# Layer 1's scores of a query pair in five score banks and one run of 1280 columns per unit, and another start for the planner's clock

## The chip, the cores and the metric

The kernel runs on one core of one Trainium2 chip. The metric is the device time of one execution in microseconds. The core has five engines that run at the same time and hand work to each other through semaphores: PE (TensorE, matmuls), DVE (VectorE), ACT (ScalarE), POOL (GpSimd) and SP (SyncE, which here issues all DMAs). PSUM, where PE writes its results, has eight banks of 512 fp32 columns by 128 partitions.

## The reference

A diffusion transformer of two layers over 1024 latent tokens and 256 context tokens, width 1024, all in fp32. Layer 0 is attention in a neighbourhood with a bias, layer 1 is full attention with 16 query heads that share 4 key and value heads; after each stands a SwiGLU block of hidden width 2816. Cut to layer 1's mixer, which the change touches:

```python
def qknorm_gqa_mixer(h_lat, h_ctx, w_qkv, q_gain, k_gain, w_o, ang_row, ang_col, with_ctx_out):
    q, k, v = project_qkv(h_lat, w_qkv, GQA_HEADS, GQA_KV_HEADS)      # 16 and 4 heads of 64
    qc, kc, vc = project_qkv(h_ctx, w_qkv, GQA_HEADS, GQA_KV_HEADS)
    q = axial_rope(rms_norm(q, q_gain), ang_row, ang_col)
    k = axial_rope(rms_norm(k, k_gain), ang_row, ang_col)
    kc = rms_norm(kc, k_gain)
    k_all = jnp.concatenate([kc, k], axis=1)                          # 256 + 1024 keys
    v_all = jnp.concatenate([vc, v], axis=1)
    ...
    s = jnp.einsum('bqhgd,bshd->bhgqs', q_b, k_all).astype(jnp.float32) * scale
    p = jax.nn.softmax(s, axis=-1).astype(v_all.dtype)
    return jnp.einsum('bhgqs,bshd->bqhgd', p, v_all)
```

Layer 1 is the last one, so its context tokens give keys and values alone.

## The kernel before

**Products in two parts.** Every operand of a matmul is split into a high part, rounded to the fast fp32r format, and a low part, the rest. A projection (`dense`, lines 782 to 784) is three matmuls per 128 input columns: high by high, high by low, low by high. The names `wh`, `wl` are the parts of a weight, `ah`, `al` those of an activation. ACT makes the high part (line 219) and POOL or DVE the low part (line 209).

**Stages.** A start-up (to about 128 us in the profile) whose order is written by hand with times; layer 0's projections, attention and output projection (to about 850 us); layer 0's SwiGLU (to 1765 us); layer 1's norm and its key and value projections; layer 1's attention (1866 to 2568 us), with the query projections and the output projection of the first 512 tokens between; layer 1's SwiGLU (to the end).

**What sets the order.** From the end of the start-up on, a planner (`Sim`) writes the program. Each piece of work is a generator that yields the letter of an engine (P, A, D, G or S) when it wants to issue. The planner has a clock of its own, a cost for each instruction (`cost`, `LAT`), a time for each engine from which it is free (`free`) and one for the DMAs (`dma_end`). It gives an engine that is free by its clock to the waiting generator of the lowest line number; the attention has lines 1 and 2, the projections come through `pump` on line 9 and so take PE when nothing of the attention wants it. `Slots.take` and `Slots.back` hand out buffers by that clock. On the chip only the order on each engine remains, and the semaphores. Before, PE counted as busy until 20 us after the planner's start (`p0=20000.0`, in ns) and the DMAs as free from its start.

**Layer 0's opening.** The planner's part begins while PE works on the last value projection of the start-up (line 716). SP then issues masks, the rows for the modulation, key and query tiles of head 0 (`K`, `Qs`, lines 1158 to 1169), `Vt`, the bias `braw`, a weight and the modulation's weights `adaw`. PE's work is the scores (line 1237), the projections of the next two heads (782 to 784), whose weights are already there, the transposes of the probabilities (1261) and the products with the values (1282). DVE adds the bias and finds the extreme (1244), and sums the modulation (752).

**Layer 1's attention.** The work is tiled into pairs: one head and 256 queries, two units of 128 queries. There are 64 pairs: two blocks of 512 queries by 16 heads by two. For a pair before:

- `ctx_scores` (1527, 1528): the scores against the 256 context keys, both units into one bank `X`, and one reduction over it for both maxima (1530).
- `scores1` (1538, 1539), twice per unit: 512 keys into a bank of `S`, of which there are two, and a reduction (1541). The query tile `Q` holds high over low; the keys lie in two tiles, high over low (`k1`) and low over high (`k2`), and the two matmuls against them give all four products.
- `unit1`: DVE takes the extreme of the three maxima (1550); ACT takes the exponential in three pieces of 512, 512 and 256, each with its sum (1556); DVE adds the three sums (1563) and inverts (1565); POOL scales the 1280 probabilities in `Pt` (1567).
- `part`, three times per unit: PE transposes 2 or 4 blocks of 128 into a bank of `T`, of which there are three (1574); ACT copies the high part into `pT` (1580); DVE subtracts for the low part (1582).
- `weigh1`: per unit ten matmuls (1605) of the values `V`, whose 128 columns are high and low part, with the 256 columns of `pT`, high beside low, into the unit's half of the one bank `o`.
- `gather` (815 to 825): ACT copies the parts on other partitions (817, 820), DVE adds in two steps (823, 825) into `z`.

The last bank, `ps`, is that of the projections. So the eight banks are three `T`, one `X`, two `S`, one `o`, one `ps`. SBUF holds two query tiles, four key tiles, two value tiles, three `Pt`, two `pT`, four `z`, two `o32`, two `xr`. After the attention `out_split` loads its output back and splits it (`ah`, `al`, lines 800 and 802), and the SwiGLU stage's first matmuls (`pm`) need all of it.

## Time and profile before

| | |
|---|---|
| median of 3 runs | 3374.49 us (3369.88 to 3377.92) |
| the profiled execution's own time | 3373.64 us |
| its span, first to last instruction | 3371.9 us |
| mean granted TensorE clock | 0.982 |
| PE, DVE, ACT, POOL busy | 94%, 58%, 40%, 29% of the span |

In the profile's rows a line such as `L1541 DVE TENSOR_REDUCE nm<-Sb ... x256 | 170.0, 684 | 59.0 <-PE ...` gives source line, engine, operation, output and inputs, count, busy time in us, mean duration of one in ns, and the engine's idle time before it with what ended it. Matmul durations overlap, so what a matmul costs is the distance between starts and not its duration. A row of the windows gives start and end, length, then for each engine busy time and count, the granted clock as a share, the share of the DMA engines and GB/s.

### The profile page before, as it was taken

The numbers are of one execution on the slowest core, as the hardware profiler recorded it, in microseconds if no ns is written. First come the engines' busy times: TensorE is split into PE (matmuls) and PEld (weight loads), VectorE is DVE, ScalarE is ACT, GpSimd is POOL, SyncE is SP. The second block draws the span as 40 slices with busy tenths as digits, with TensorE's granted clock in tenths as the row PEclk, the third lists the DMA queues.
The fourth block names the chain that finished last, engine by engine and source line by source line (L and its number), as shares of the span: only waits on it lengthen the run. The fifth ranks groups of instructions, "written<-read, shape, count | busy, mean of one in ns | idle before, by whom it ended". The sixth has DMA issues, their size and how long they took to land. (4 is left out here: it accounts for less than half of the span.)

```text
span 3371.9 us, 47168 instructions
## 1 busy us (share of the span) xinstructions
PE 3157.7 (94%) x17352; PEld 2690.8 (80%) x17352; DVE 1949.0 (58%) x3843; ACT 1335.5 (40%) x2915; POOL 968.4 (29%) x807
## 2 busy tenths in 40 slices
PE   7699999988999999999998998889887999999998
PEld 5688899867888888888886777678776788888887
DVE  7587975655665533333365777887887333333335
ACT  4254555543311111111134777777775311211223
POOL 4243543343211011000035554324334211110112
PEclk8899999999999999999999999999999999999999
DMA  7766755554333311111115233213211211111111
GB/s 242 209 198 200 225 177 167 173 163 151 122 119 120 127 39 38 38 42 40 38 39 179 93 119 88 57 56 93 74 49 60 75 44 38 63 50 38 49 57 57
DMA packets 177591, 337.98 MB, mean 100 GB/s; under 512 B 29904, under 2 KB 80336, under 8 KB 175312
## 3 DMA queue, kind: packets, MB, share of 16 engines
q1 hardware_dynamic: 177360, 334.96, 31.6%
q8 instruction: 137, 2.24, 0.3%
q14 instruction: 94, 0.77, 0.1%
HBM read 267.78 MB, written 70.64 MB: 100 GB/s over the span
## 5 line engine op out<-in xcount | busy, mean ns | idle before, releaser
L209 POOL TENSOR_TENSOR wl<-wr,wh 128x512 fp32r<-128x512 f32 x214 | 293.7, 1378 | 1186.4 <-ACT wh L219 1182.1
L956 ACT ACTIVATE sa<-pa 128x512 f32<-128x512 f32 (+1 forms) x110 | 61.0, 555 | 734.3 <-PE pa L784 734.2
L993 PE MATMUL pm<-hh,woh 128*128 128x512 f32 (+1 forms) x912 | 330.1, 362 | 0.0
L994 PE MATMUL pm<-hl,woh 128*128 128x512 f32 (+1 forms) x912 | 329.5, 361 | 0.0
L995 PE MATMUL pm<-hh,wol 128*128 128x512 f32 (+1 forms) x912 | 329.3, 361 | 0.0
L1004 DVE SCALAR_TENSOR_TENSOR h<-pm,modB,h 128x512 f32<-128x512 f32 (+1 forms) x368 | 242.1, 662 | 148.1 <-PE pm L995 147.6
L783 PE MATMUL pa<-al,wh 128*128 128x512 f32 (+1 forms) x880 | 324.9, 369 | 2.9 <-POOL al L336 1.8
L782 PE MATMUL pg<-ah,wh 128*128 128x512 f32 (+1 forms) x880 | 325.1, 369 | 0.0
L782 PE MATMUL pa<-ah,wh 128*128 128x512 f32 (+1 forms) x880 | 325.0, 369 | 0.0
L784 PE MATMUL pa<-ah,wl 128*128 128x512 f32 (+1 forms) x880 | 324.5, 369 | 0.0
L783 PE MATMUL pg<-al,wh 128*128 128x512 f32 (+1 forms) x880 | 324.4, 369 | 0.0
L784 PE MATMUL pg<-ah,wl 128*128 128x512 f32 (+1 forms) x880 | 324.0, 368 | 0.0
L219 ACT CAST wh<-wr 128x512 fp32r<-128x512 f32 x334 | 203.5, 622 | 255.6 <-PE pg L783 101.9
L970 DVE TENSOR_TENSOR sa<-sa,pg 128x512 f32<-128x512 f32 (+1 forms) x110 | 69.6, 633 | 365.6 <-PE pg L784 365.5
L1567 POOL TENSOR_SCALAR Pt<-Pt,rc 128x1280 f32<-128x1280 f32 x128 | 177.4, 1386 | 327.4 <-PE Tb L1574 231.0
L1605 PE MATMUL ob<-pT,V 128*128 128x256 f32 x1280 | 202.3, 296 | 55.1 <-DVE z L825 21.0
L752 DVE CUSTOM_DVE_ANT_0 adaj<-adaw,crow 128x512 f32<-128x512 f32 x256 | 207.9, 812 | 73.3 <-DMA adaw<-in_adaT 70.9
L209 DVE TENSOR_TENSOR wl<-wr,wh 128x512 fp32r<-128x512 f32 x120 | 96.1, 803 | 265.4 <-ACT wh L219 265.0
L1605 PEld LDWEIGHTS ob<-pT,V 128*128 128x128 f32 x1280 | 169.7, 191 | 83.1 <-ACT pT L1580 25.4
L1580 ACT CAST pT<-Tb 128x512 fp32r<-128x512 f32 (+1 forms) x384 | 182.8, 521 | 103.1 <-PE Tb L1574 99.4
L1582 DVE TENSOR_TENSOR pT<-Tb,pT 128x512 fp32r<-128x512 f32 (+1 forms) x384 | 212.0, 590 | 6.8 <-ACT pT L1580 4.1
L1541 DVE TENSOR_REDUCE nm<-Sb 128x1 f32<-128x512 f32 x256 | 170.0, 684 | 59.0 <-PE Sb L1539 58.6
(273 smaller groups left out, 7693.0 us busy)
## 6 DMA issues: line engine op xcount, KB each, us to landing
wr<-in_fin SPq DMA_DIRECT2D x88, 512.0 KB, 3.5
adaw<-in_adaT SPq DMA_DIRECT2D x160, 256.0 KB, 3.7
wr<-in_wqkv SPq DMA_DIRECT2D x53, 512.0 KB, 4.6
wr<-in_fout SPq DMA_DIRECT2D x44, 512.0 KB, 3.5
wr<-in_wo SPq DMA_DIRECT2D x32, 512.0 KB, 4.0
K<-Kd SPq DMA_DIRECT2D x32, 320.0 KB, 5.5
Qs<-Qd SPq DMA_DIRECT2D x80, 128.0 KB, 4.3
Vt<-Vd SPq DMA_DIRECT2D x16, 640.0 KB, 5.7
```

The costliest lines, as they stand in the source:

```text
L209: (g if self.engine == "G" else v).tensor_tensor(lo[:, c], raw[:, c], hi[:, c].bitcast(F32), ALU.subtract)
L219: s.copy(hi[:, c], raw[:, c])
L752: v.tensor_tensor_reduce(junk[:], aw[:], crow[w][:, c * 512:c * 512 + 512], 1.0, 0.0, ALU.mult, ALU.add, raw[:, m, w, c:c + 1])
L782: t.matmul(ps, lhsT=hi[:, c], rhs=ah[:, kc, :n], start=kc == 0, stop=False)
L783: t.matmul(ps, lhsT=hi[:, c], rhs=al[:, kc, :n], start=False, stop=False)
L784: t.matmul(ps, lhsT=lo[:, c], rhs=ah[:, kc, :n], start=False, stop=kc == KC - 1)
L993: t.matmul(ps[:, :n], lhsT=hi[:, c], rhs=hh[:, cols], start=i == 0, stop=False)
L994: t.matmul(ps[:, :n], lhsT=hi[:, c], rhs=hl[:, cols], start=False, stop=False)
L995: t.matmul(ps[:, :n], lhsT=lo[:, c], rhs=hh[:, cols], start=False, stop=i == 1)
L1004: v.scalar_tensor_tensor(h, ps[:, :n], self.g2(m, b), h, ALU.mult, ALU.add)
L1582: v.tensor_tensor(pT[:, i0:i0 + n, P:], Tv, pT[:, i0:i0 + n, :P].bitcast(F32), ALU.subtract)
L1605: t.matmul(o[:, p * 256:p * 256 + 256], lhsT=pair.hd.kv.V[:, kb, :], rhs=pT[:, i, :], start=i == 0, stop=i == 9)
```

## The change

It has two parts.

*The planner's start.* `p0` becomes 3000 and `d0`, new, tells the planner that the DMAs are taken up to 15 us after its start.

*Layer 1's attention.* One tile `S5` of five banks holds a pair's scores. Columns 0 to 1023 are unit 0's own keys, 1024 to 1279 its context keys, 1280 to 1535 unit 1's context keys, 1536 to 2559 its own keys, so that each unit has a run of 1280 columns and the middle bank holds the context scores of both. One reduction and one exponential with its sum serve a unit. The planner treats the tile as three parts: `scores_[0]` and `scores_[1]` are given back after the exponential of their unit, `scores_[2]`, the middle, after the second. The query tile now holds high over low and low over high side by side, and the key tile exists once; the two matmuls take the two query copies against the same keys. The other three banks, `B`, serve transposes, results, projections and the means of the norms; a projection takes one during the attention only where two are idle. Transposes put both units' high parts side by side and their low parts beside them (`pT`, and `pt` for the last two blocks), and the product adds high and low side in the same 256 columns, 2 matmuls per block of keys, 20 per pair as before; it begins when all six pieces of both units are there. The gather is one copy and one addition. Before layer 1's attention its projections use the five banks one by one (`banks["S"]`).

```diff
-CFG = dict(lag=3, tv=8.0, tm=5.0, t1=43.0, t2=58.0, p0=20000.0)
+CFG = dict(lag=3, tv=8.0, tm=5.0, t1=43.0, t2=58.0, p0=3000.0, d0=15000.0)
...
         bg.free.update(P=CFG["p0"])
+        bg.dma_end = CFG["d0"]
...
+    def bank1():
+
+        slots = banks["B" if live["att"] else "S"]
+        while len(slots.idle) < (2 if live["att"] else 1):
+            yield ""
+        return slots, slots.idle.pop(0)
...
+                    pair.S = yield from scores_[0].take()
+                    bg.enter("att", own_scores(pair, 0), 1)
+                    yield from scores_[2].take()
                     bg.enter("att", ctx_scores(pair), 1)
+                    yield from scores_[1].take()
+                    bg.enter("att", own_scores(pair, 1), 1)
                     for p in range(2):
+                        bg.enter("att", unit1(pair, p), 2)
                     bg.enter("att", weigh1(pair), 2)
 
+    def scores1(pair, p, d, sl):
+        for i in range(2):
+            t.matmul(pair.S[:, d:d + sl.stop - sl.start], lhsT=pair.q[p][:, i], rhs=pair.hd.kv.k[:, sl], start=i == 0, stop=i == 1)
...
+    def unit1(pair, p):
+        S = pair.S[:, 1280 * p:1280 * p + 1280]
...
         yield "D"
+        v.tensor_reduce(rc[:, 0:1], S, AX.X, ALU.max, negate=True)
         Pt = yield from A1["Pt"].take()
+        yield "A"
+        s.activation(Pt[:], S, AF.Exp, bias=rc[:, 0:1], accum_out=rc[:, 1:2])
+        scores_[p].back(pair.S)
         pair.x -= 1
         if not pair.x:
+            scores_[2].back(pair.S)
...
+        T = yield from banks["B"].take()
...
+        hi = pT[:, :, p * P:p * P + P]
+        yield "A"
+        s.copy(hi, Tv)
+        yield "D"
+        v.tensor_tensor(pT[:, :, 256 + p * P:256 + p * P + P], Tv, hi.bitcast(F32), ALU.subtract)
+        banks["B"].back(T)
...
+        while len(pair.got) < 6:
+            yield ""
+        o = yield from banks["B"].take()
+        for c, (k0, k1) in enumerate(TURN1):
+            pT = pair.pT[c]
+            for k in range(k0, k1):
+                yield "P" if k == 9 else "P0"
+                for j in range(2):
+                    t.matmul(o[:, 0:256], lhsT=pair.hd.kv.V[:, k, :], rhs=pT[:, k - k0, 256 * j:256 * j + 256],
+                             start=k + j == 0, stop=k + j == 10)
...
+        s.copy(ob[mine], o[other, 0:256])
+        yield "D"
+        v.tensor_tensor(z[mine], o[mine, 0:256], ob[mine], ALU.add)
+        banks["B"].back(o)
...
-    for name, n in (("T", 3), ("X", 1), ("S", 2), ("o", 1), ("ps", 1)):
-        banks[name] = Slots(many(pp, n, name + "b", [P, 512]))
+    S5 = pp.tile([P, 2560], F32, name="S5")
+    scores_ = [Slots([S5]) for _ in range(3)]
+    banks["S"] = Slots([S5[:, i * 512:i * 512 + 512] for i in range(5)])
+    banks["B"] = Slots(many(pp, 3, "Bb", [P, 512]))
...
+          (("K", 2, LAT + CTX, F32R), ("Pt", 4, 1280, F32), ("ob", 2, 256, F32), ("z", 3, 256, F32),
+           ("o32", 1, 512, F32), ("xr", 1, 512, F32))}
     A1["V"] = Slots(many(pb, 2, "V_", [P, 10, P], F32R))
-    A1["pT"] = Slots(many(pb, 2, "pT_", [P, 10, 2 * P], F32R))
+    A1["Q"] = Slots(many(pb, 2, "Q_", [P, 2, 512], F32R))
+    A1["pT"] = Slots(many(pb, 3, "pT_", [P, 4, 512], F32R))
+    A1["pt"] = Slots(many(pb, 2, "pt_", [P, 2, 512], F32R))
```

What the built program's order shows, first on PE at the opening of layer 0: `S_` are score banks of layer 0, `ps_` projections, `K`, `Qs` the loaded keys and queries. Before:

```order
L716 MATMUL ps_1089<-vl_174,ah_675 128x256
L1237 MATMUL S_1130<-K_1138,Qs_1135 128x256 x4
L1237 MATMUL S_1131<-K_1138,Qs_1135 128x384 x2
L1237 MATMUL S_1131<-K_1138,Qs_1135 128x256 x2
L782 MATMUL ps_1133<-ah_302,wh_68 128x512
```

In the changed program 96 matmuls of projections stand between that first row and the scores; this is their end on PE:

```order
L782 MATMUL ps_1134<-ah_302,wh_66 128x512
L783 MATMUL ps_1134<-al_303,wh_66 128x512
L784 MATMUL ps_1134<-ah_302,wl_67 128x512
L1237 MATMUL S_1130<-K_1138,Qs_1135 128x256 x4
L1237 MATMUL S_1131<-K_1138,Qs_1135 128x384 x2
L1237 MATMUL S_1131<-K_1138,Qs_1135 128x256 x2
```

The scores of head 0 moved behind the key projection of the next two heads (1280 columns) and the first 512 columns of their query projection.

The second place is one pair on PE in the middle of layer 1's attention, where no projection stands between. Before (`Xb`, `Sb` scores, `Tb` transposes, `ob` the result):

```order
L1527 MATMUL Xb_14049<-K_14590,Q_14586 128x256
L1528 MATMUL Xb_14049<-K_14591,Q_14586 128x256
L1538 MATMUL Sb_14051<-K_14590,Q_14586 128x512
L1539 MATMUL Sb_14051<-K_14591,Q_14586 128x512
L1538 MATMUL Sb_14050<-K_14590,Q_14586 128x512
L1539 MATMUL Sb_14050<-K_14591,Q_14586 128x512
L1574 MATMUL Tb_14046<-ident,Pt_14593 128x128 x2
L1574 MATMUL Tb_14047<-ident,Pt_14593 128x128 x4
L1605 MATMUL ob_14052<-pT_14608,V_14605 128x256 x10
```

Now (`S_14046` is the tile of five banks, the `Bb_` are the three others):

```order
L1603 MATMUL Bb_14048<-pt_14603,V_14595 128x256 x4
L1520 MATMUL S_14046<-K_14582,Q_14597 128x512 x2
L1580 MATMUL Bb_14049<-ident,Pt_14586 128x128 x4
L1520 MATMUL S_14046<-K_14582,Q_14597 128x512 x2
L1580 MATMUL Bb_14049<-ident,Pt_14586 128x128 x2
L1580 MATMUL Bb_14047<-ident,Pt_14587 128x128 x4
L1520 MATMUL S_14046<-K_14582,Q_14597 128x256 x4
L1520 MATMUL S_14046<-K_14582,Q_14597 128x512 x4
L1580 MATMUL Bb_14049<-ident,Pt_14587 128x128 x2
L1603 MATMUL Bb_14047<-pT_14601,V_14595 128x256 x8
```

Transposes of the pair before now stand between the scores of a pair, and the results take turns on the three banks instead of one. In the whole attention, from the first transpose to the last product, 429 projection matmuls stand between where 528 did, in smaller portions, and 120 stand behind its end where none did.

The third place is DVE in the same stretch. Before (`nm`, `rc` hold maxima, sums and inverses):

```order
L1530 TENSOR_REDUCE nm<-Xb_14049 128x2
L1541 TENSOR_REDUCE nm<-Sb_14051 128x1
L1541 TENSOR_REDUCE nm<-Sb_14050 128x1
L1582 TENSOR_TENSOR pT_14608<-Tb_14048,pT_14608 128x4x128
L1550 TENSOR_REDUCE rc<-nm 128x1
L1582 TENSOR_TENSOR pT_14607<-Tb_14046,pT_14607 128x2x128
```

Now, with the semaphores that each instruction waits for:

```order
L1546 TENSOR_REDUCE rc<-S_14046 128x1 [waits PE_49,Pool_49]
L1588 TENSOR_TENSOR pt_14602<-Bb_14049,pt_14602 128x2x128 [waits Activation_49]
L1546 TENSOR_REDUCE rc<-S_14046 128x1 [waits Pool_49]
L1588 TENSOR_TENSOR pT_14600<-Bb_14048,pT_14600 128x4x128 [waits Activation_49]
L1555 RECIPROCAL rc<-rc 128x1 [waits Activation_49]
```

Two reductions per pair stand where five and four small ones stood, and the second waits for no semaphore of ACT.

More of the change, by code (lines that the diff above doesn't have):

```diff
@@ L1418, in finish_qk1 @@
         s.activation(sq[:, :n], x[:, :n], AF.Square)
-        ms = yield from banks["T"].take()
+        ms = yield from banks["B"].take()
         yield "P"
@@ L1425, in finish_qk1 @@
         s.activation(rs[:, :n], ms[:, :n], AF.Ln, bias=eps[:])
-        banks["T"].back(ms)
+        banks["B"].back(ms)
         yield "A"
@@ L1587, in unit1, with turn1 @@
-        for i0, n in ((0, 2), (2, 4), (6, 4)):
-            T = yield from banks["T"].take()
-            bg.enter("att", part(i0, n, T), 2)
-        while len(left) < 3:
-            yield ""
-        pair.done[p] = u
+        yield ""
+        pair.done[p] = Pt
+        for c in range(3):
+            bg.enter("att", turn1(pair, p, c), 1)
+    TURN1 = (0, 4), (4, 8), (8, 10)
+    def turn1(pair, p, c):
+        k0, k1 = TURN1[c]
+        n = k1 - k0
+        Pt = pair.done[p]
+        if c not in pair.pT:
+            pair.pT[c] = None
+            pair.pT[c] = yield from A1["pT" if n == 4 else "pt"].take()
+        while pair.pT[c] is None:
+            yield ""
+        T = yield from banks["B"].take()
+        pT, Tv = pair.pT[c], T[:, :n * P].rearrange("p (i q) -> p i q", q=P)
+        yield "P"
+        for i in range(n):
+            k = (k0 + i + 2 * p) % 10
+            t.transpose(T[:, i * P:(i + 1) * P], Pt[:, k * P:(k + 1) * P], ident[:])
+        pair.turned[p] += 1
+        if pair.turned[p] == 3:
+            A1["Pt"].back(Pt)
+        hi = pT[:, :, p * P:p * P + P]
[4 more added lines that the diff above has]
+        banks["B"].back(T)
+        yield ""
+        pair.got.add((p, c))
@@ L1594, in weigh1 @@
     def weigh1(pair):
         h, b = pair.h, pair.b
-        o = yield from banks["o"].take()
-        blocks = [8, 9] + list(range(8))
-        for p in range(2):
-            while pair.done[p] is None:
-                yield ""
-            pT = pair.done[p].pT
-            for i, kb in enumerate(blocks):
-                if i in (0, 5):
-                    yield "P" if i else "P0"
-                t.matmul(o[:, p * 256:p * 256 + 256], lhsT=pair.hd.kv.V[:, kb, :], rhs=pT[:, i, :], start=i == 0, stop=i == 9)
-            A1["pT"].back(pT)
+        while len(pair.got) < 6:
+            yield ""
```

128 lines of the change are left out of this document (38 added, 90 removed).

## The prediction

> **What bounds the kernel now.** The page comes first: the span, and the busy share of each engine.
>
> ```profile
> span 3371.9 us, 47168 instructions
> PE 3157.7 (94%) x17352; PEld 2690.8 (80%) x17352; DVE 1949.0 (58%) x3843; ACT 1335.5 (40%) x2915; POOL 968.4 (29%) x807
> ```
>
> TensorE is busy 94% of the span, but a busy PE is not a PE at its pace. So the second view is the windows, here the two feed-forward stages (each row: start and end, length, then busy time and count by engine, granted clock, DMA):
>
> ```profile
> 850.00:1700.00 850.00, 850.00 (x4444) 732.81 (x4443) 384.39 (x697) 148.32 (x263) 103.46 (x76) 1.00 0.21 71
> 2640.00:3340.00 700.00, 697.14 (x3079) 575.92 (x3078) 251.17 (x329) 141.64 (x238) 106.66 (x79) 1.00 0.14 47
> ```
>
> Here PE never waits, and the rows give its pace: 700 / 3079 = 0.227 us for a matmul of 512 columns. In the earlier stage a third of them have 256 columns: (850 - 2963 x 0.227) / 1481 = 0.120 us. Nothing in the change can win there. The third view is the same table for layer 1's attention, then for line 782 alone (one matmul in three of a projection) and for line 1567 alone (one per unit of 128 queries, two to a pair):
>
> ```profile
> 1866.00:2055.00 189.00, 177.44 (x960) 145.03 (x960) 148.72 (x298) 139.21 (x329) 115.08 (x85) 0.97 0.34 107
> 2055.00:2247.00 192.00, 159.38 (x1054) 134.21 (x1052) 160.64 (x387) 146.89 (x388) 59.57 (x45) 0.99 0.23 62
> 2247.00:2398.00 151.00, 144.40 (x922) 126.74 (x920) 118.99 (x279) 107.99 (x287) 58.00 (x44) 1.00 0.32 97
> 2398.00:2568.00 170.00, 141.89 (x946) 119.02 (x945) 141.30 (x343) 129.99 (x344) 52.67 (x39) 1.00 0.13 37
> ```
>
> ```profile
> 1866.00:2055.00 189.00, 48.14 (x114) 21.28 (x113) 0.97 0.34 107
> 2055.00:2247.00 192.00, 0.00 (x0) 0.00 (x0) 0.99 0.23 62
> 2247.00:2398.00 151.00, 27.09 (x64) 12.08 (x64) 1.00 0.32 97
> ```
>
> ```profile
> 1866.00:2055.00 189.00, 34.83 (x24) 0.97 0.34 107
> 2055.00:2247.00 192.00, 55.27 (x41) 0.99 0.23 62
> 2247.00:2398.00 151.00, 38.51 (x29) 1.00 0.32 97
> 2398.00:2568.00 170.00, 48.83 (x36) 1.00 0.13 37
> ```
>
> A transpose's pace comes from two rows of the timeline:
>
> ```profile
> 2095.93 0.82 PE L1574 MATMUL Tb<-ident,Pt 128*128 128x128 f32 x6
> ...
> 2099.33 0.60 PE L1574 MATMUL Tb<-ident,Pt 128*128 128x128 f32 x4
> ```
>
> (0.82 - 0.60) / 2 = 0.11 us. A pair is 8 matmuls of 512, 24 of 256 and 20 transposes: 1.82 + 2.88 + 2.18 = 6.88 us of PE. Without projections (2055 to 2247) a pair takes 192 / 20.5 = 9.37 us, 1.36 times that. With them (2247 to 2398) the work is 14.5 x 6.88 + 192 x 0.227 = 143 us in 151, 1.05 times; in the first stretch 82.6 + 342 x 0.227 = 160 in 189, 1.18 times. So projections fill PE's gaps, and where they run out PE waits for this:
>
> ```profile
> PE ob L1605 <- DVE z L825: 21.0, 20, 1.2
> PE ob L1605 <- DVE z L823: 11.7, 20, 0.6
> PE ob L1605 <- DVE rc L1550: 11.0, 34, 0.5
> ```
>
> VectorE stands behind each, busy 160.64 of 192 us, 84%. The pure stretches are a chain of three nearly full engines on single buffers (one result bank, two score banks).
>
> **The change, part by part.** The rows that price the softmax:
>
> ```profile
> L1541 DVE TENSOR_REDUCE nm<-Sb 128x1 f32<-128x512 f32 x256 | 170.0, 684 | 59.0 <-PE Sb L1539 58.6
> L1530 DVE TENSOR_REDUCE nm<-Xb 128x2 f32<-128x512 f32 x64 | 44.1, 689 | 34.9 <-PE Xb L1528 34.8
> L1249 DVE TENSOR_REDUCE rc<-S 128x1 f32<-128x256 f32 x32 | 13.2, 416 | 3.7 <-PE S L1237 3.6
> L1550 DVE TENSOR_REDUCE rc<-nm 128x1 f32<-128x3 f32 x128 | 18.7, 146 | 1.1
> L825 DVE TENSOR_TENSOR z<-ob,z 64x256 f32<-64x256 f32 x64 | 28.4, 444 | 1.2
> L823 DVE TENSOR_TENSOR z<-ob,ob 64x256 f32<-64x256 f32 x64 | 26.7, 417 | 3.3 <-ACT ob L817 2.2
> L1556 ACT ACTIVATE Pt<-Sb,rc 128x512 f32<-128x512 f32 x256 | 173.8, 685 | 27.7 <-DVE rc L1550 24.9 <-POOL Pt L1567 0.3
> L1556 ACT ACTIVATE Pt<-Xb,rc 128x256 f32<-128x256 f32 x128 | 60.5, 473 | 0.0
> L1556 ACT ACTIVATION_READ_ACCUMULATOR Pt<-Sb,rc 128x1 f32 x256 | 50.6, 198 | 0.0
> L1580 ACT CAST pT<-Tb 128x512 fp32r<-128x512 f32 (+1 forms) x384 | 182.8, 521 | 103.1 <-PE Tb L1574 99.4
> ```
>
> *VectorE, per pair.* Gone: four reductions at 684, one at 689, four small ones (4 x 146, taking line 1563 like 1550), two sums at 417 and 444: 4.87 us. New: one sum (0.43) and two reductions over 1280. No row shows that width; from 256 to 512 columns the row grows by 268 ns, so 684 + 3 x 268 = 1488 ns; bounds are 2.5 x 684 = 1710 above and, for a flat cost per column below, 684 + 768 x 0.8 = 1300. I take 1488, the straight line through both rows: 3.41 us, 1.46 less. Busy time counts overlapping ends once, so of 160.64 / 20.5 = 7.84 us a pair 6.4 to 6.8 stay.
>
> *ScalarE, per pair.* Six exponentials with their reads (4 x 685 + 2 x 473 + 6 x 198 = 4.87 us) become two over 1280: 685 + 3 x 212 = 1321 each, 2 x (1321 + 198) = 3.04. It saves 1.8 us, and is off the bound: worth nothing by itself. POOL's work per pair stays.
>
> *PE* issues the same columns in every group (query copies instead of key copies; high and low side by side): 0. Per head SP issues three query loads instead of two and per key head two fewer key loads; both are hidden, since a head's two pairs take over 14 us and there are two query tiles. If that cover were gone, a landing of 3.3 us would stand 32 times, 106 us:
>
> ```profile
> Q<-Q1d SPq DMA_DIRECT2D x64, 128.0 KB, 3.3
> ```
>
>  One residual tile and one output tile fewer cost PE nothing while projections stand in order behind them.
>
> *Banks and waits.* One result bank, three transpose banks, one projection bank and three score banks become five score banks, held by one pair, and three for all else. New waits: the next pair's first scores wait for this pair's first exponential, its context scores for the second. Queued behind on PE are transposes and products, and nobody else waits longer. The loop through the scores, with nothing in front, is context scores 0.48, two reductions 2.98, the second exponential 1.52, some 0.4 of handing over: 5.4 us, shorter than PE's 6.88, if not by much.
>
> So the stage: PE's floor is 64 x 6.88 + projections. The built order has 429 projection matmuls inside it instead of 528, and spreads them (some 9 to 24 to two pairs, where before runs of none alternate with 72): 440 + 97 = 538 us. If VectorE stays at 84% it allows 6.6 / 0.84 = 7.9 us a pair, 503 in all; with the projections wholly on top that is 600, with 6.8 it is 613. Between 538 (all hidden) and 613 (none) I take the middle, 575, since the filled stretches of before lie at 1.05 and 1.18 and this is 1.07. Before it is 702. **Term: -127** (-164 to -89).
>
> The 99 projection matmuls that left are done elsewhere: 120 more behind the last attention matmul, 21 fewer ahead, 99 x 0.227: **+22.5**. Behind the end they cover these waits for the last output block (**-2.7**, at worst 0):
>
> ```profile
> 2575.26 0.50 PE L782 MATMUL pm<-ah,wh 128*128 128x512 f32 x1 [1.82 <-ACT ah L800]
> 2576.61 0.50 PE L783 MATMUL pm<-al,wh 128*128 128x512 f32 x1 [0.85 <-POOL al L802]
> ```
>
> *The planner's clock* (p0, d0) moves layer 0's opening:
>
> ```profile
> 115.45 0.28 PE L716 MATMUL ps<-vl,ah 128*128 128x256 f32 x1
> 129.15 2.38 PE L1237 MATMUL S<-K,Qs 128*128 128x256 f32 x8 [13.42 <-DMA Qs<-Qd]
> 131.75 0.63 PE L783 MATMUL ps<-al,wh 128*128 128x512 f32 x1
> 132.17 0.63 PE L784 MATMUL ps<-ah,wl 128*128 128x512 f32 x1
> 149.17 1.12 PE L1261 MATMUL S<-ident,Pt 128*128 128x128 f32 x4 [12.18 <-POOL Pt L1257]
> 120.00:140.00 20.00, 7.85 (x27) 6.45 (x27) 4.76 (x8) 1.14 (x2) 4.95 (x4) 0.66 1.03 286
> ```
>
> PE stands 13.42 us for the queries and 12.18 for the first scaled probabilities; around that the clock is 0.66 and a matmul takes 0.42 instead of 0.227. Now 96 projection matmuls stand first, 72 x 0.227 + 24 x 0.120 = 19.2 us, until 135; the queries landed at 129. The first transposes then wait some 2 us. Gone 25.6 plus some 3 of slow clock, less 2, less 4 for waits that come later in another order: **-22** (0 to -29). Late in layer 0, where its projections run out, the order looks as before, so I expect the lead to last. Everything else keeps its instructions: 0, give or take 8.
>
> Sum: -22 - 127 + 22.5 - 2.7 = -129. The profiled execution took 3373.64 us, 1.7 more than its span and 0.9 under the median of the three runs. 3373.6 - 129 = 3244.6, so **3245**.
>
> **The rivals.**
> *Opening worth nothing* (the attention still waits on VectorE and the DMAs behind it): 3373.6 - 107 = 3267. For it: DMA at 1.03 of its engines in that window.
> *PE's floor*: stage at 538, opening -22: 3373.6 - 164 - 2.2 = 3208. For it: spread projections; against it: every stretch of before lies above 1.05.
> *The old ratio*: three near-full engines stall as now, 702 / 560 = 1.25 (560 = 440 + 528 x 0.227): 538 x 1.25 = 673, 3373.6 - 29 - 2.2 = 3342.
> *Slower: the score banks are a serial loop.* All five belong to one pair. If VectorE's other 3.6 us a pair (6.6 less 2.98) queue ahead of the reductions and ScalarE's six copies (6 x 0.521) ahead of the exponentials, 5.4 becomes 12.1 a pair: 776 instead of 702, 3373.6 + 74 - 2.2 = 3445. It decides from 11.0 us a pair, (702 + 2.2) / 64. Against it: in 60 of 64 pairs the order sets at most three other instructions between the two reductions.
> *The shared bank.* The middle bank holds both units' context scores; if one engine's reading had to end before the other's began, the second reduction waits out an exponential, 1.5 us a pair on VectorE: 6.6 + 1.5 = 8.1, / 0.84 = 9.6, 617 alone and 665 with half the projections: 3373.6 - 37 - 2.2 = 3334. The built program puts no semaphore of ScalarE on that reduction. The Trainium skill speaks for this rival: PSUM — Partial Sum Buffer, section "PSUM bank collisions raise a hardware error", wants every two engines' accesses to one bank and partition quadrant ordered, reads too. No run here shows it.
> *The edits cancel or do not act*: 3373.
>
> **How the numbers follow.** Forecast within its terms 0.60; opening nothing 0.10; floor 0.10; old ratio 0.09; shared bank 0.03; serial loop 0.04; no change 0.04. The range takes the first three: 3205 (floor, all terms good, less a little) to 3305 (613 with no gain at the opening, 3373.6 - 89 + 20 = 3305). About 0.2%, 7 us, can be told from no change. Faster 0.92, same 0.04, slower 0.04.
>
> **What would show it.** In the changed profile: PE's wait for Qs and for the first Pt under 5 us together and its clock near 1.0 from 120 to 160; the stretch from the first to the last transpose of layer 1 near 575 us; reductions of 1280 near 1.49 us, exponentials near 1.32; VectorE near 6.6 us a pair; some 27 us of projections after the last product. Wrong would be: a pair at 9.4 us again, a PE that mostly waits for exponentials (the serial loop), or a reduction that waits for one.

## The result, and the profile after

The changed kernel takes **3401.38 us** (median of 4 runs, 3399.95 to 3403.84), the kernel before beside it 3375.05: a ratio of 1.008, with an interval of 1.0063 to 1.0098. It is 0.8% slower; the forecast was 3245. The profiled execution took 3399.95 us.

The page's first lines, span and busy share of each engine:

```profile
span 3398.2 us, 45937 instructions
PE 3167.5 (93%) x17352; PEld 2689.8 (79%) x17352; DVE 1870.6 (55%) x3316; ACT 1266.7 (37%) x2403; POOL 986.8 (29%) x822
```

VectorE and ScalarE have work taken off them (1949.0 and 1335.5 us before), TensorE's busy time is up by only 10 us (3157.7 before), and the span is 26 us longer. So somebody waits more. First the part that went as forecast, the opening (windows, columns as before):

```profile
120.00:140.00 20.00, 19.21 (x106) 16.47 (x104) 6.83 (x16) 4.87 (x11) 6.16 (x6) 1.00 1.03 322
```

PE is busy 19.21 of 20 us (7.85 before) at a clock of 1.00 (0.66). By starts in the timeline, the first score matmul of layer 1 comes at 1829.6 us, before at 1854.5: 25 us ahead. The attention then ends at 2571.6, before at 2568.3: between its first score and its last product lie 742.0 us against 713.8. From the first transpose, as the prediction counts, it is 730 (1841.4 to 2571.6) against its 702, and 575 was forecast. The lead is gone there, and the projections that were left over come behind the end as foreseen: from the last product to the end 826.6 us against 803.6.

The groups by shape (duration as mean ns of one, then the idle time before them):

```profile
L1546 DVE TENSOR_REDUCE rc<-S 128x1 f32<-128x1280 f32 x128 | 188.3, 1487 | 63.8 <-PE S L1520 47.7 <-ACT Pt L1549 15.8 <-issue 0.2
L1549 ACT ACTIVATE Pt<-S,rc 128x1280 f32<-128x1280 f32 x128 | 170.6, 1333 | 70.4 <-DVE rc L1546 36.6 <-PE S L1520 29.0 <-DVE rc L1555 2.3
L1549 ACT ACTIVATION_READ_ACCUMULATOR Pt<-S,rc 128x1 f32 x128 | 25.1, 196 | 0.0
L1520 PE MATMUL S<-K,Q 128*128 128x512 f32 x512 | 164.6, 431 | 82.1 <-DVE rc L1546 46.0 <-ACT Pt L1549 34.9 <-ACT pT L1586 0.6
```

The durations are those forecast: 1487 ns (1488) and 1333 (1321). The last column isn't: PE stands 82.1 us in front of the scores, 46.0 of them **for a reduction**. No wait of that kind was in the forecast's list: a reduction only reads scores. And 15.8 us of the reductions' idle time end with an exponential, 29.0 of the exponentials' with a score matmul, though an exponential follows a reduction that has already waited for its scores. These are three waits that the data don't ask for. The timeline shows one, in rows of PE, DVE and ACT that touch the scores of a pair (the row with x6 is four context matmuls and the first two own ones of unit 1):

```profile
2090.60 1.20 PE L1520 MATMUL S<-K,Q 128*128 128x256 f32 x6 [0.22 <-ACT Pt L1549]
...
2091.91 1.49 DVE L1546 TENSOR_REDUCE rc<-S 128x1 f32<-128x1280 f32 x1 [1.17 <-PE S L1520]
...
2093.45 0.73 PE L1520 MATMUL S<-K,Q 128*128 128x512 f32 x2 [1.22 <-DVE rc L1546]
...
2094.84 1.48 DVE L1546 TENSOR_REDUCE rc<-S 128x1 f32<-128x1280 f32 x1
...
2097.62 1.33 ACT L1549 ACTIVATE Pt<-S,rc 128x1280 f32<-128x1280 f32 x1
```

Unit 0's reduction needs the four context matmuls, but starts at 2091.91, after unit 1's first own scores as well (1.20 us from 2090.60). Unit 1's next scores go into a bank that the reduction doesn't read; they start at 2093.45, when it has ended (2091.91 + 1.49 = 2093.40). The built program says so with its semaphores: each access to the tile `S5` waits for every earlier access of another engine to that tile, whatever columns either touches, reads for reads too. 37 of the 768 score matmuls wait on a reduction, 53 of the 128 exponentials on score matmuls that come later than those they read, 38 exponentials on the other unit's reduction, 12 of the reductions on an exponential. The 37 and the 53 share no bank with what they wait for; the 38 and the 12 share only the middle one, with other columns.

### The profile page after: what moved, and what is told of

Its sections match the earlier page's. It is cut to its first block, busy times and chain, and to the rows that moved or that the text cites. A ratio compares the mean times of both kernels' runs of the same rounds, so it can differ in the third digit from the quotient of the medians.

```text
span 3398.2 us, 45937 instructions
## 1 busy us (share of the span) xinstructions
PE 3167.5 (93%) x17352; PEld 2689.8 (79%) x17352; DVE 1870.6 (55%) x3316; ACT 1266.7 (37%) x2403; POOL 986.8 (29%) x822
## 5 line engine op out<-in xcount | busy, mean ns | idle before, releaser
L209 POOL TENSOR_TENSOR wl<-wr,wh 128x512 fp32r<-128x512 f32 x219 | 305.0, 1399 | 1236.3 <-ACT wh L219 1236.2
L1520 PE MATMUL S<-K,Q 128*128 128x512 f32 (+1 forms) x768 | 203.3, 393 | 86.7 <-DVE rc L1546 46.0
L209 DVE TENSOR_TENSOR wl<-wr,wh 128x512 fp32r<-128x512 f32 x115 | 88.2, 770 | 266.3 <-ACT wh L219 266.1
L1580 PE MATMUL Bb<-ident,Pt 128*128 128x128 f32 x1280 | 200.8, 281 | 31.4 <-DVE pT L1588 28.1
L1546 DVE TENSOR_REDUCE rc<-S 128x1 f32<-128x1280 f32 x128 | 188.3, 1487 | 63.8 <-PE S L1520 47.7
L1580 PEld LDWEIGHTS Bb<-ident,Pt 128*128 128x128 f32 x1280 | 155.1, 144 | 79.6 <-issue 44.1
L1520 PEld LDWEIGHTS S<-K,Q 128*128 128x128 f32 x768 | 121.7, 200 | 121.6 <-DVE rc L1546 56.2
```

Of the source, the lines that this page charges most:

```text
L209: (g if self.engine == "G" else v).tensor_tensor(lo[:, c], raw[:, c], hi[:, c].bitcast(F32), ALU.subtract)
L1520: t.matmul(pair.S[:, d:d + sl.stop - sl.start], lhsT=pair.q[p][:, i], rhs=pair.hd.kv.k[:, sl], start=i == 0, stop=i == 1)
L1580: t.transpose(T[:, i * P:(i + 1) * P], Pt[:, k * P:(k + 1) * P], ident[:])
```

## The experiments

**The theories.** *Whole tile*: the five banks are one object to the program's waits, so that scores, reductions and exponentials of a pair and the next are strung on one line, which the planner, with its three parts, knows nothing of. *One set of scores*: the next pair must truly wait for this pair's banks. *Shared bank*: the middle one. *Small banks*: three for transposes, sums and projections, where there were five. *Longer runs*: the shorter work of VectorE and ScalarE is what can gain. *Pieces awaited* and *order*: when a sum begins, and what the planner puts first.

Each ratio is to the kernel before that ran beside it (3373.12 to 3375.12 us). The last column has the start of layer 1's first score matmul in the profile, and the time from there to the last product.

| run | median us | ratio to before (interval) | first score at, to the last product |
|---|---|---|---|
| before | 3375.05 | 1 | 1854.5, 713.8 |
| changed | 3401.38 | 1.008 (1.0063 to 1.0098) | 1829.6, 742.0 |
| opening | 3345.06 | 0.9911 (0.9896 to 0.9926) | 1818.8, 715.2 |
| one6 | 3525.83 | 1.0448 (1.0430 to 1.0465) | 1833.0, 854.8 |
| two6 | 3451.20 | 1.0227 (1.0212 to 1.0242) | 1827.6, 784.3 |
| split5 | 3351.13 | 0.9931 (0.9917 to 0.9946) | 1829.1, 718.5 |
| split_b2 | 3465.41 | 1.0272 (1.0255 to 1.0289) | 1825.5, 800.4 |
| c2b5 | 3367.61 | 0.9982 (0.9969 to 0.9994) | 1813.1, 746.0 |
| c2b3 | 3430.89 | 1.0165 (1.0150 to 1.0180) | 1814.8, 807.1 |
| c3b4 | 3359.83 | 0.9953 (0.9938 to 0.9968) | 1822.0, 736.2 |
| h1b5 | 3381.31 | 1.0018 (1.0009 to 1.0028) | 1824.0, 749.5 |
| split5_pre | 3341.46 | 0.9903 (0.9888 to 0.9917) | 1818.0, 715.8 |
| split5_five | 3330.13 | 0.9873 (0.9855 to 0.9891) | 1816.8, 700.7 |
| split5_early | 3348.23 | 0.9919 (0.9902 to 0.9935) | 1819.7, 717.3 |
| c2b5_t2 | 3361.39 | 0.9966 (0.9955 to 0.9977) | 1817.0, 737.5 |
| five_t2 | 3341.89 | 0.9909 (0.9895 to 0.9924) | 1815.5, 683.3 |
| five_u1 | 3436.60 | 1.0184 (1.0167 to 1.0201) | 1817.5, 797.0 |

The last column alone is not the price of the attention, because the planner does not put the same number of projection matmuls inside it; what it leaves out stands behind the end. By line 782, one matmul in three, there are 558 inside in the kernel before and in opening, 444 in the changed one, 405 in one6, two6 and split_b2, 378 in five_t2, 474 in five_u1, and 564 in all others. The windows from the first score to the last product, of before, changed, split5, c2b5, c2b3 and five_t2 (columns as before):

```profile
1854.50:2568.30 713.80, 634.20 (x3917) 533.60 (x3918) 574.77 (x1313) 528.83 (x1357) 287.94 (x212) 0.99 0.25 76
1829.60:2571.60 742.00, 622.81 (x3803) 518.13 (x3804) 495.80 (x780) 453.00 (x836) 294.18 (x223) 0.97 0.25 73
1829.10:2547.60 718.50, 639.12 (x3924) 529.73 (x3925) 557.81 (x1113) 485.98 (x1102) 301.53 (x223) 0.99 0.28 80
1813.10:2559.10 746.00, 637.99 (x3924) 545.26 (x3925) 544.09 (x1243) 511.98 (x1358) 301.63 (x223) 0.97 0.26 77
1814.80:2621.90 807.10, 678.77 (x3923) 557.15 (x3924) 544.31 (x1236) 517.02 (x1358) 302.03 (x228) 0.94 0.24 71
1815.50:2498.80 683.30, 602.61 (x3738) 503.69 (x3739) 537.96 (x1034) 475.82 (x1021) 289.13 (x214) 0.98 0.26 75
```

### The opening alone

```diff
-CFG = dict(lag=3, tv=8.0, tm=5.0, t1=43.0, t2=58.0, p0=20000.0)
+CFG = dict(lag=3, tv=8.0, tm=5.0, t1=43.0, t2=58.0, p0=3000.0, d0=15000.0)
...
         bg.free.update(P=CFG["p0"])
+        bg.dma_end = CFG["d0"]
```

> The kernel before with the change's first part alone: the planner is told p0=3000 and the clock of the transfers is set to 15000 before attention 0; layer 1 is the old one. If the first part is worth what the stages of the two traces say (the last product of layer 0 ended at 724.1 us before and at 692.6 after, the first FFN matmul stood at 851.0 and at 816.0), it gives 31 to 35 us to the end: 3340 to 3346, against 3375 before; the attention of layer 1 then costs 55 to 61 us more than it did, not 127 less as forecast. If layer 1 gives the time back in another way, because it has fewer projections left to fill gaps with, this run stands at 3370 to 3380 and the loss isn't the new scores' own.

3345.06 beside 3375.12: 30 us, held to the end. So the new attention costs 56 us (3401.38 - 3345.06) where the forecast had it gain 107 (-127 + 22.5 - 2.7).

### One tile or two

Of the changed kernel, with six banks for scores and two small ones; first one tile, then the same split in two:

```diff
-    S5 = pp.tile([P, 2560], F32, name="S5")
+    S5 = pp.tile([P, 3072], F32, name="S5")
...
-        S = pair.S[:, 1280 * p:1280 * p + 1280]
+        S = pair.S[:, 1792 * p:1792 * p + 1280]
...
-    banks["B"] = Slots(many(pp, 3, "Bb", [P, 512]))
+    banks["B"] = Slots(many(pp, 2, "Bb", [P, 512]))
```

> The changed kernel with the scores of a pair in ONE tile of six banks instead of five, each unit in three banks of its own, so that no bank is shared; two banks instead of three for transposes, weighed sums and projections. Theory (whole tile): the program makes every read and write of the scores wait for all earlier ones of the same tile, whatever banks they touch, so banks of their own change nothing; with one small bank less it is as slow as the changed kernel or slower, 3400 to 3480. Rival (shared middle bank): the units hinder each other in the bank that holds both context parts; then it is 30 or more below 3401. Rival (too few small banks): 60 or more above 3401, by the small banks alone.

```diff
-    S5 = pp.tile([P, 3072], F32, name="S5")
+    S5 = many(pp, 2, "S5", [P, 1536])
...
-        S = pair.S[:, 1792 * p:1792 * p + 1280]
+        S = pair.S[p][:, 256 * p:256 * p + 1280]
```

> The same as the run before it, instruction by instruction in the same order on TensorE, with the six banks as TWO tiles of three, one for each unit. Nothing but the waits differs. Theory (whole tile): TensorE's waits of the scores for reductions and exponentials (85 us in the changed kernel, 46.0 and 39.4) go for the most part, and it is 50 to 90 us faster than the run with one tile. Rival (one set of scores is simply too little: the next pair's scores must wait for this pair's exponentials, a true dependency): within 10 us of the run with one tile. Rival (small banks): within 15 us, since two small banks bind both.

3525.83 (above its theory's 3400 to 3480) and 3451.20: where the tile ends is worth **75 us**. On all five engines the two programs have the same instructions in the same order, on the same sizes; only semaphores differ. The view of line 1520, what its engine waited for and who waited for it (us, times), with one tile:

```profile
its engine sat idle before it (us, times) until:
  ACT Pt L1549: 108.0, 165
  DVE rc L1546: 40.1, 26
  DMA Q<-Q1d: 14.5, 13
  issue: 1.5, 4
who waited for it (us, times):
  DVE rc L1546: 31.8, 60
  ACT Pt L1549: 24.0, 53
```

And with two:

```profile
its engine sat idle before it (us, times) until:
  ACT Pt L1549: 20.0, 62
  DMA Q<-Q1d: 12.3, 11
  issue: 2.0, 7
who waited for it (us, times):
  DVE rc L1546: 2.5, 4
```

The three waits that the data don't ask for are gone (scores for a reduction 40.1 to nothing, exponentials for later scores 24.0 to nothing, and in the view of line 1546 reductions for an exponential 2.6 to nothing). The scores' waits for exponentials fall from 108.0 to 20.0 (weight loads counted in): with one tile 60 of the 114 semaphores for them were for an exponential that reads other banks, with two all 119 are for the one that frees the bank. So one set of scores costs little here for a true reason. The shared bank is not the cause of the larger waits either: one6 shares none between the units and has them all the same. It is 124 us *slower* than the changed kernel; that is put down to the third small bank, which was taken away with it, since in two6 PE waits elsewhere, in transposes and products that need a small bank's subtraction done:

```profile
PE Bb L1603 <- DVE pT L1588: 78.6, 59, 1.6
PE Bb L1580 <- DVE pT L1588: 32.8, 79, 2.4
```

### Five banks as three tiles

```diff
-    S5 = pp.tile([P, 2560], F32, name="S5")
+    S5 = [pp.tile([P, n], F32, name=f"S5{i}") for i, n in enumerate((1024, 1024, 512))]
...
+        v.tensor_reduce(rc[:, 1:2], pair.S[p][:], AX.X, ALU.max, negate=True)
+        v.tensor_tensor(rc[:, 0:1], rc[:, 1:2], pair.nm[:, p:p + 1], ALU.min)
...
+        s.activation(Pt[:, 256 * p:256 * p + 1024], pair.S[p][:], AF.Exp, bias=rc[:, 0:1], accum_out=rc[:, 3:4])
+        s.activation(Pt[:, 1024 - 1024 * p:1280 - 1024 * p], pair.S[2][:, 256 * p:256 * p + 256], AF.Exp, bias=rc[:, 0:1], accum_out=rc[:, 4:5])
```

> The changed kernel with five banks of scores as THREE tiles: own scores of unit 0 (1024 columns), own scores of unit 1, and the context of both (512); three small banks as in the changed kernel. A reduction runs over 1024 and one over both contexts, an exponential over 1024 and one over 256, with a least and a sum of two columns: about 1.0 us of VectorE and 0.9 us of ScalarE more for a pair. Theory (whole tile): 40 to 100 us faster than the changed kernel, 3300 to 3360, in spite of more instructions. Rival (one set of scores): the added work lengthens the same loop, 3400 to 3460. Rival (small banks): as many as in the changed kernel, so 3390 to 3460.

3351.13, **50 us faster than the changed kernel with more instructions**: the whole tile again. This pair is less clean than the last, for the planner's order is another: 120 projection matmuls that stood behind the attention stand inside it again. The attention is 23.5 us shorter in spite of them (742.0 to 718.5) and what follows it 21.5 (826.6 to 805.1). But split5 is only level with the old attention (3345): without those waits the change's second part is worth nothing, not 107. What is late next stands in the waits of PE:

```profile
PE Bb L1588 <- DVE pT L1596: 26.3, 45, 1.7
PE S L1520 <- ACT Pt L1553: 21.4, 25, 1.9
PE Bb L1611 <- DVE pT L1596: 11.6, 17, 1.5
```

Twice it is small banks (`Bb`), once the scores' true wait. To see what the longer runs are worth, the same with the small banks of two6:

```diff
-    banks["B"] = Slots(many(pp, 3, "Bb", [P, 512]))
+    banks["B"] = Slots(many(pp, 2, "Bb", [P, 512]))
```

> The run with three tiles of scores (runs of 1024 and 256), with two small banks instead of three. It has the small banks of the run with two tiles of runs of 1280 (3451), and 1.0 us more of VectorE and 0.9 us more of ScalarE for a pair, 64 and 58 us in all. If those engines' work is on the path, as the forecast's 22 to 64 us for the longer runs had it, it stands at 3470 to 3515; theory (the longer runs' own gain is hidden beside banks and waits): 3440 to 3465.

3465.41, at the edge of the two: runs of 1280, together with a middle bank that is not shared, save 14 us (3451.20), where the expectation counted 122 of engine work. By busy time the difference is smaller, 53 us on DVE and 37 on ACT (1932.3 and 1297.3 in split_b2, 1879.7 and 1260.7 in two6), and most of that is hidden. It also shows 114 us (3465 - 3351) for the third small bank, 82 of them in the attention and the rest behind it, where 159 more projections then stand.

### Small banks

The scores as before (banks of 512 that go back singly, a bank for the contexts), new gathering, five small banks, then three, two left empty; four with one more for the scores; and the two score banks as one tile of 1024:

```diff
-    S5 = pp.tile([P, 2560], F32, name="S5")
+    Sb, Xb = many(pp, 2, "Sb", [P, 512]), pp.tile([P, 512], F32, name="Xb")
...
-    banks["B"] = Slots(many(pp, 3, "Bb", [P, 512]))
+    banks["B"] = Slots(many(pp, 5, "Bb", [P, 512]))
```

> The changed kernel with the scores taken as the kernel before takes them (two banks of 512 columns that go back singly, one for both contexts, reductions over 512, three exponentials for a unit), and FIVE small banks; the new gathering of hi and lo of both units stays. VectorE has about 0.9 us more for a pair than with runs of 1280, ScalarE about 1.5. Theory (small banks): the transposes, sums and projections that wait for one of three small banks are, beside the waits of the whole tile, what the change lost; with five the new gathering pays: 3270 to 3330. Rival (runs of 1280 are what the change gains by): with runs of 512 it is no better than the first part alone, 3340 to 3380.

> The same as the run before it with THREE small banks in place of five, two banks left empty; not one instruction more or less. Theory (small banks): 40 to 110 us slower than with five (a third bank taken away cost 125 us: 3526 for one tile of six banks and two small ones, against 3401). Rival (three are enough, and only two are too few): within 10 us of the run with five.

> As with five small banks, with one of them given to the scores: three banks of 512 for own scores, one for the contexts, FOUR small ones. Theory (small banks): slower than five by 10 to 40 us, between the runs with five and three. Rival (the scores are short of banks): faster than five by 10 or more.

> As with five small banks, but the two banks of own scores are one tile of 1024 columns: one reduction and one exponential over 1024 for a unit and one of 256 for the context, and a unit's first scores wait for the whole of the unit before it. VectorE and ScalarE have 0.7 to 1.2 us less work for a pair than with runs of 512. Theory (order of the two engines and TensorE in one set of scores): the loop of a unit is 0.9 us of scores, 1.2 of reduction, 1.3 of exponential and the handing over, 4.0 to 4.5 us, 8 to 9 for a pair, under the present 9.3 to 10.5 but with nothing beside it in that bank: 3300 to 3370, 10 to 50 slower than with runs of 512. Rival (instructions on VectorE and ScalarE bind): 10 to 40 faster than with runs of 512.

Three for five costs **63 us** (3430.89 - 3367.61), as the theory had it. The instructions are the same, but the planner spreads some elementwise ones otherwise over VectorE and GpSimd, and the order differs. The waits of PE, with five and with three:

```profile
PE Sb L1522 <- ACT Pt L1555: 95.5, 43, 3.6
PE Bb L1590 <- POOL Pt L1567: 9.7, 29, 1.5
```

```profile
PE Bb L1590 <- DVE pT L1598: 49.0, 50, 2.6
PE Sb L1522 <- ACT Pt L1555: 24.0, 38, 3.8
PE Bb L1590 <- DVE rc L1551: 18.9, 31, 1.1
PE Bb L1590 <- POOL Pt L1567: 15.2, 20, 1.9
```

With three, transposes wait for a bank; with five, that wait is gone, and the scores wait for exponentials instead. These waits are not all of the 63 us. By the windows above the attention is 61 us longer with three; PE stands idle 20 of these more, and is busy 41 more with the same matmuls, at a mean granted clock of 0.94 against 0.97. The clock alone would make 637.99 x 0.97 / 0.94 = 658 of the busy time, an estimate, so about half of the 41. The step to four is not seen: c3b4, with one more score bank, is 8 us *faster* than five (the theory had it slower, the rival faster by 10), so the eight banks have no easy place left. h1b5 is 14 slower than c2b5, as the theory had it (its time, 3300 to 3370, it missed with c2b5): fewer, longer instructions don't pay for banks that come back later. And c2b5 missed: 3368 where the theory had 3270 to 3330, and inside the 3340 to 3380 of its rival. With the old scores and as many banks as before, what is left of the second part, mainly the new gathering, stands 22 us *behind* the old attention (3345).

### Ahead of the attention, and five turns

The projections before the attention used five slices of one tile. In split5 with a slice of each tile only, then also with the last two blocks of both units turned together, then also with the sum begun early:

```diff
-    banks["S"] = Slots([S5[i // 2][:, i % 2 * 512:i % 2 * 512 + 512] for i in range(5)])
+    banks["S"] = Slots([S[:, 0:512] for S in S5])
```

> The run with three tiles of scores, with one edit ahead of the attention: the projections that are made before it take three banks, one of each tile, instead of five, two of which share a tile. Theory (whole tile): two projections whose halves lie in one tile wait for each other's reading; the attention began at 1829.1 us there and at 1813.1 where every bank was its own tile, so it begins 8 to 16 us earlier, and the time is 3335 to 3344 against 3351. Rival (fewer banks cost): two banks less make the projections wait, 3355 to 3370.

```diff
+    def tail1(pair):
...
+        for i in range(2):
+            for p in range(2):
+                k = (8 + i + 2 * p) % 10
+                t.transpose(T[:, (2 * i + p) * P:(2 * i + p + 1) * P], pair.done[p][:, k * P:(k + 1) * P], ident[:])
...
+        s.copy(hi, Tv)
+        v.tensor_tensor(pt[:, :, 256:512], Tv, hi.bitcast(F32), ALU.subtract)
```

> The run before it with the last two blocks of both units turned together in one small bank: five turns for a pair in place of six, one copy and one subtraction of 512 columns for two of 256. Theory (small banks): a sixth less of them is asked for, and 0.3 us less of both engines for a pair: 8 to 30 us faster than the run before it, 3310 to 3335, under the 3345 of the first part alone. Rival (the later unit binds): the first unit's last blocks wait for the second unit, its buffer stays longer, and it is the same within 6 us or slower.

```diff
-        while len(pair.got) < 6:
+        while not {(0, 0), (1, 0)} <= pair.got:
             yield ""
         o = yield from banks["B"].take()
         for c, (k0, k1) in enumerate(TURN1):
+            while not {(0, c), (1, c)} <= pair.got:
+                yield ""
```

> The run before it, with the weighed sum begun when the first piece of both units is there, not all of them. Rival (pieces awaited): the sum's twenty matmuls stand in the gaps of the pieces that follow, 5 to 20 us faster than the run before it. Theory (small banks): the sum's bank is held while the other pieces still need banks, so it is the same or up to 25 us slower.

3341.46, 3330.13 and 3348.23. Fewer banks, but each a tile, are 10 us faster: the whole tile once more, ahead of the attention (it begins at 1818.0, not 1829.1). One turn less for a pair gives 11. To hold a small bank for the sum while pieces still come costs 18, so waiting for all pieces was no loss; a scarce bank is a reading that fits, as transposes wait 11.7 us for a subtraction there, against 3.1. **split5_five at 3330.13 beats both kernels**, by 1.3% the one before and by 2.1% the changed one. In the attention its PE now waits for scores' banks first:

```profile
PE S L1520 <- ACT Pt L1553: 33.9, 23, 2.0
PE Bb L1590 <- POOL Pt L1565: 13.3, 17, 1.7
PE Bb L1610 <- DVE pT L1598: 12.3, 21, 1.4
```

### The planner's order

Turns a line lower (2, as in the kernel before) in c2b5 and in split5_five, and then reductions and exponentials a line higher:

```diff
-            bg.enter("att", turn1(pair, p, c), 1)
+            bg.enter("att", turn1(pair, p, c), 2)
```

> The run with two banks of 512 for scores and five small banks, with the turns put a line lower in the planner (2 instead of 1, as the kernel before has them), so that reductions and exponentials go first. Theory (order): the wait of the scores for exponentials falls from 95 us to under 50, and the time by 15 to 40, to 3330 to 3352, level with the first part alone (3345). Rival (the pair's own loop: both units must be turned before a product of the pair starts): within 8 us of 3368.

> The version with five turns for a pair, three tiles and three small banks (3330), with its turns a line lower, level with reductions and exponentials. Theory (order): 5 to 20 us faster, 3310 to 3325. Rival (small banks): the turns that hold small banks go on later and give them back later: the same or up to 25 us slower.

```diff
-                        bg.enter("att", unit1(pair, p), 2)
+                        bg.enter("att", unit1(pair, p), 1)
```

> The run before it, with reductions and exponentials a line higher, ahead of the turns. Theory (order): as that run or up to 10 us faster. Rival (small banks): slower than 3330 by 5 to 30 us.

c2b5_t2 is 3361.39, within its rival's 8 us of 3368. The scores' wait falls from 95.5 to 15.2 us, but the time by only 6: the transposes now wait for POOL's scaling.

```profile
PE Bb L1590 <- POOL Pt L1567: 56.1, 40, 2.6
PE Sb L1522 <- ACT Pt L1555: 15.2, 17, 1.5
PE Xb L1522 <- ACT Pt L1558: 14.7, 20, 0.8
```

So this order makes 6 of the 22 us and mostly changes who is waited for. five_t2 (12 slower) and five_u1 (106 slower, far beyond the 30 expected at most) both lose. five_t2 has the shortest attention of all, 683.3 us, and loses behind it: 186 projection matmuls fewer stand inside than in split5_five, and what follows takes 841.6 us against 804.1. In five_u1 the waits say where, in transposes that wait until an addition gives the sum's bank back:

```profile
PE Bb L1590 <- DVE z L1646: 50.8, 50, 2.1
```

## Why the prediction was wrong

**Opening, -22:** right, and larger: -30 measured alone, just beyond the 0 to -29 given for it.

**Sizes of instructions:** right. 1487 and 1333 + 196 ns against 1488 and 1321 + 198; VectorE has 78 us less in all (1949.0 - 1870.6), 1.2 us a pair, against 1.46. What failed is that they count: 14 us between two6 and split_b2 is all that longer runs gave there, an unshared middle bank counted in, with the same two small banks and no false waits between the units' own scores.

**"New waits: the next pair's first scores wait for this pair's first exponential, its context scores for the second."** This step failed. I took the three parts that the planner gives back for the waits that the program makes. The program makes them by tile. The loop through the scores was then not 5.4 us but all of a pair's accesses in a row: scores 4 x 2 x 0.227 + 4 x 0.120 = 2.3, reductions 2 x 1.49, exponentials 2 x 1.53, 8.3 us before any handing over and any other work in between; the pair took 730 / 64 = 11.4. With a tile for each part 3401 becomes 3351, and 3341 with that ahead of the attention too. That is all of the loss against opening (3345), but of the 163 us between the -107 forecast for this part and the +56 measured it is only 60. The other 100 or so are not explained by it.

**"The built program puts no semaphore of ScalarE on that reduction":** true of the pair whose order was shown, wrong in general. 12 of the 128 reductions have one.

**"Three for all else"** was told and not priced: the stage was worked out from PE's floor and VectorE's share, as if banks came free when asked for. It is the second step that failed: 63 us between three and five small banks with the old scores, 114 between two and three with three tiles. VectorE, reckoned at 84%, was busy 67% of the changed attention (495.80 / 742.00) and 78% in split5. Without false waits the attention stays at its old length (718.5 against 713.8) and not near 575; that small banks and the gathering hold it there is a reading that fits, for no run has the scores' tiles and more than three small banks.

**Projections moved, +22.5 - 2.7:** right. The 120 matmuls behind the end alone are 120 x 0.227 - 2.7 = 24.5, and 23.0 more were measured from the last product to the end.

**The rivals.** *The serial loop* (3445, from 11.0 us a pair, chance 0.04) had sign and threshold right, 11.4 a pair, but another mechanism: instructions queued ahead, where one6 and two6 show semaphores. Its chance was small because I went by the order of the instructions and not by what each waits for. The queue is not ruled out beside them: in the pair shown above the first exponential starts at 2097.62, 4.2 us after its reduction's end, behind copies and norms on ScalarE, and no run prices that in the changed kernel. *The shared bank* is real but small: the wait that it names, a reduction for an exponential, ends 15.8 us of VectorE's idle time; the larger waits stand in one6 too, which shares no bank, and split5 still shares it and is 50 us faster. The Trainium skill, PSUM — Partial Sum Buffer, section "PSUM bank collisions raise a hardware error", asks for order between engines by bank and quadrant, reads included; the program orders more than that, and no run here leaves such an order out, so none tests the rule. Of the waits counted above the 38 and the 12 are of the kind that it asks for, the 37 and the 53 are not. *Old ratio* (3342) is where the kernel stands once each part of the scores is a tile of its own: 3341. Its ratio held: with 440 us for the attention's own matmuls and 0.227 for each projection inside, 713.8 / 567 = 1.26 before and 715.8 / 568 = 1.26 in split5_pre. That the two times agree to 1 us is luck: the opening gave 8 us more than it counted, the second part 6 less. Its reason, three nearly full engines, no run showed.

**Left open:** why the attention without false waits is no shorter than the old one, and why the new gathering, with old scores and five small banks, is 22 us behind the old, 16 with the old planner lines. PE's wait moves between exponentials and POOL with the planner's lines, so that the loop of a pair whose two units must both be turned is a reading that fits; no run showed it.

## What to carry to other kernels

What waits for what is settled by the program's objects, not by the columns: before counting on banks that are "given back" one by one, look in the built program at whom each access waits for, and make each part that is used alone a tile of its own. A wait of a writer for an engine that only reads other columns (here 46.0 us of scores for reductions) is the sign of it in a profile. And price the banks that a change takes away as well as the instructions: here instructions saved on two engines gave 14 us, and two banks cost 63 with the old scores.

## What the runs showed beyond the forecast

Nothing new of the hardware itself. The new sizes ran within 1% of the straight line through the old ones (1487 ns for 1488, 1333 for 1321). The mean granted clock of the profiled executions stayed between 0.974 and 0.991, but inside the attention it was lower in slower versions: 0.99 before and in split5, 0.97 in the changed kernel, 0.94 in c2b3. By the estimate above that is about half of the busy time added in c2b3; no run separates it from the waits. The surprises were the program's waits and how steeply the time climbs with the last small bank: 63 us for the step from five to three with the old scores, 114 for that from three to two with three tiles.
